# Log-sum-exp over heads: the range check as a chain of reduces, and a new split of the heads of a whole tile

## The chip, the cores and the metric

The kernel runs on one core of a Trainium2 chip. The engines are named TensorE (PE in the profile, with PEld for its weight loads), VectorE (DVE), ScalarE (ACT), GpSimd (POOL) and SyncE (SP, which here only starts transfers). The metric is the device time of one execution in microseconds. Three runs of the kernel before gave 335.59, 335.64 and 335.72 us, so the median is 335.64 us.

## The reference

```python
def reference(x, bias):                       # x (8, 2048, 2048) f32, bias (8, 256) f32
    B, S, D = x.shape
    H = bias.shape[0]
    Dh = D // H
    x_heads = x.reshape(B, S, H, Dh).transpose(0, 2, 1, 3)
    x_heads = x_heads + bias[None, :, None, :]
    x_tiled = np.repeat(x_heads, 2, axis=2)
    mx = x_tiled.max(axis=-1, keepdims=True)
    lse = mx.squeeze(-1) + np.log(np.exp(x_tiled - mx).sum(axis=-1))
    return lse.astype(np.float32)
```

For each of the 16384 rows and 8 heads, the 256 numbers of the head get the head's bias, and the logarithm of the sum of their exponentials is wanted; every result is written twice side by side. The input is 134.2 MB and the output 1.05 MB, so nearly all traffic is the load of `x`.

The kernel sums exp(x + bias) without taking the maximum away first. A range check makes that safe: it looks whether every sum lies within a factor of 2^60 of one, and whether no bias is larger than 20 in size. If the check fails, a slow second pass (`all_again`) computes everything with the maximum; on this input the pass is skipped.

## The kernel before

**Tiles and buffers.** The work is cut into 64 tiles, eight per batch. A tile is two rows on each of 128 partitions: 128 x 2 x 2048 numbers, 2.1 MB. Four buffers `xb` hold two tiles each. Tiles 2 to 41 are loaded two at a time (4.2 MB, line 171), the others one at a time or in pieces (line 183), all by SP's queue in the order of the tiles. A buffer is loaded again once the last instructions that use it (`last_uses`) are done, so a load eight tiles ahead waits for a tile to be finished.

**Stages.** `STAGES` says how the heads of a tile are shared out. Tiles 0 to 53 are whole tiles in the mode `BULK`; tiles 54 to 56 are `MIXED`; tiles 57 to 63 are worked on in half tiles and smaller pieces.

**A whole tile** (`BULK`: `pe=3, acc=1, g0=4`) goes three ways:
- Heads 0 to 2: TensorE writes the bias into PSUM (`put_bias`, line 297: a matmul of ones with three bf16 parts of the bias) and adds `x` to it with a matmul by the identity (`late_heads`, line 356). ScalarE takes the exp. For head 0 it also sums (line 367, `one_ps`); heads 1 and 2 are written back to SBUF (line 374, `pair`).
- Head 3: ScalarE takes the exp of the bare `x`, and VectorE multiplies by exp(bias), which lies in PSUM in `w_ps` (line 424, 2 x 256 numbers a partition).
- Heads 4 to 7: GpSimd adds the bias in SBUF (`g_add`, line 406, 2 x 1024 numbers), and ScalarE takes the exp.

One exp on ScalarE covers heads 3 to 7 (`exp_inplace`, line 412, 2560 numbers). At the end one `tensor_reduce` on VectorE sums heads 1 to 7 of both rows (line 431, 3584 numbers into 14 sums). The sums of a batch land in a tile `R` (128 partitions x 128 numbers).

**Weighing** (`weigh`, line 447) is another form: one fused VectorE instruction multiplies a head of one row by exp(bias) and sums it, and a second, short one reads the sum out of the accumulator. Before the change only the mixed and the last tiles use it. In the last tiles GpSimd multiplies and folds one or two heads (`fold`, lines 463 and 471), and TensorE runs spare matmuls (`keep_warm`, line 347).

**Order.** The order of the instructions on each engine is the order in which the program emits them (`manual_schedule`). The loop over tiles emits TensorE's and GpSimd's part of tile t, then the second half of tile t-1 (`later`: exp, multiply, reduce, reload), then ScalarE's exps of the heads of tile t that TensorE made (`pe_part`).

**End of a batch.** One iteration after the batch's last sums, `finish` transposes `R` on TensorE (line 491) and ScalarE takes the logarithm (line 501). `how_far` checks the sums on VectorE: a `tensor_scalar` takes the bits of the sums as integers less the bits of 1.0 (line 512), and a `tensor_reduce` finds the largest absolute value (line 519). After the last batch `judge` reduces the nine columns of `far`, turns the column into a row with TensorE and reduces it to one number, which all engines read to decide on the second pass.

Of the kernel before, what the change touches and what calls it, by code (L numbers as in the profile page):

```python
# [11 lines left out]
I32 = mybir.dt.int32  # L12
# [20 lines left out]

BULK = dict(pe=3, acc=1, g0=4, late=True, fold=0)
MIXED = dict(pe=1, acc=1, g0=4, late=False, fold=0)
# [9 lines left out]
SPAN_BITS = 60 << 23  # L45
TOO_FAR = float(1 << 30)

# [15 lines left out]
def kernel(  # L63
# [37 lines left out]

    far = sb.tile([P, B + 1], F32, name="far")
    dist = sb.tile([P, P], F32, name="dist")
    b_far = sb.tile([1, 1], F32, name="b_far")
    all_far = sb.tile([P, 1], F32, name="all_far")
    verdict = sb.tile([1, 1], I32, name="verdict")

    R = [sb.tile([P, KB, H, NB], F32, name=f"R{b}") for b in range(B - 1)]
    R_last = sb.tile([P, H, NBLK, K], F32, name="R_last")
    res = sb.tile([H * NB, B - 1, P, KB, 2], F32, name="res")  # L110
# [125 lines left out]
    for i, c in enumerate(range(G0, D, MM)):  # L236
        spread(ps[i], c, c + MM)
        nc.vector.tensor_copy(b_rep[:, c - G0 : c - G0 + MM], ps[i])
    w_late = w_ps[:, 0 : G0 - W0]
    spread(w_late, W0, G0)  # L240
    nc.scalar.activation(out=w_late, in_=w_late, func=ACT.Exp)

    nc.vector.memset(far, 0.0)
    nc.vector.tensor_reduce(
# [6 lines left out]
    nc.vector.tensor_scalar(  # L251
        out=far[0:1, B : B + 1],
        in0=b_far,
# [10 lines left out]
    def other_factors():  # L264
        nc.scalar.activation(
            out=w_ps[:, G0 - W0 :], in_=b_rep[:, 0 : W2 - G0], func=ACT.Exp
        )
        nc.scalar.activation(out=w_sb, in_=b_rep[:, W1 - G0 :], func=ACT.Exp)
# [81 lines left out]

    def late_heads(m, t, got, sums):

# [12 lines left out]
        def pe_part():  # L365
# [14 lines left out]
            )  # L380
            on_x(t, act, [mms[-1]])

# [30 lines left out]

    def later(m, t, k0, k1, sums, add):

        h0 = m["pe"] if m["late"] else m["g0"]
        v = xts[t % NBUF][:, k0:k1, h0 * Dh : D]
        done = exp_inplace(t, v, add)
        if m["late"]:
            n = (m["g0"] - h0) * Dh  # L420
            f = v[:, :, 0:n]
            h0 = m["acc"]
            v = xts[t % NBUF][:, k0:k1, h0 * Dh : D]
            mul = nc.vector.tensor_tensor(  # L424
                out=f,
                in0=f,
                in1=each_row(w_ps, m["pe"] * Dh - W0, n, k1 - k0),
                op=ALU.mult,
            )
            done = on_x(t, mul, [done])  # L430
        red = nc.vector.tensor_reduce(  # L431
            out=sums[:, k0:k1, h0:H],
            in_=v.rearrange("p k (h j) -> p k h j", j=Dh),
            op=ALU.add,
            axis=mybir.AxisListType.X,
        )
        last_uses[t].append(on_x(t, red, [done]))

# [20 lines left out]
    def fold(t, k, h0, h1, sums, after):  # L459
# [49 lines left out]

    def how_far(b, sums):  # L510

        nc.vector.tensor_scalar(  # L512
            out=dist,
            in0=sums.bitcast(I32),
            scalar1=float(ONE_BITS),
            scalar2=None,
            op0=ALU.subtract,
        )
        nc.vector.tensor_reduce(  # L519
            out=far[:, b : b + 1],  # L520
            in_=dist,
            op=ALU.max,
            axis=mybir.AxisListType.X,
            apply_absolute_value=True,
        )

    def judge():
        nc.vector.tensor_reduce(
            out=all_far, in_=far, op=ALU.max, axis=mybir.AxisListType.X
        )  # L530
        row = w_ps[0:1, 0:P]
# [96 lines left out]
    for t in range(T):  # L628
# [74 lines left out]
    finish_last()  # L703
    how_far(B - 1, R_last.rearrange("p h n k -> p (h n k)"))
    again = judge() > SPAN_BITS
# [34 lines left out]
```

## Time and profile before

| what | value |
| --- | --- |
| median of three runs | 335.64 us |
| the profiled execution's own time | 335.89 us |
| its span | 334.0 us |
| mean granted TensorE clock | 0.895 of full speed |
| loads of x (queue q1): share of 16 engines' span | 95.5% |
| line 431, reduce of 3584 numbers: count, mean | 54, 3888 ns |
| line 424, multiply of 512 numbers: count, mean | 54, 678 ns |
| line 512, tensor_scalar of the check: count, mean | 7, 2640 ns |
| line 519, reduce of the check: count, mean | 8, 286 ns |
| line 406, GpSimd's add of 2048 numbers: count, mean | 57, 4536 ns |
| line 412, exp of 2560 numbers: count, mean | 54, 2346 ns |

The profile is of one execution. A row of a group gives its line, engine and operation, the tile written and the tile read, shapes, count, total and mean busy time, and the idle time of the engine ahead of it with what ended it. A row of the windows gives a stretch of the span, then for each engine the busy time and the number of instructions, then the granted TensorE clock, the busy share of the 16 DMA engines and the rate of the transfers. In the slices each digit is a fortieth of the span in tenths of busy time. The busy times of two neighbouring instructions on VectorE or ScalarE may overlap a little, so the distance from one start to the next is the better price of an instruction in a row of them.

### The profile page before, as it was taken

What the parts mean: (1) busy time and instruction counts of PE and PEld (TensorE: products, weight loads), DVE (VectorE), ACT (ScalarE), POOL (GpSimd) and SP (SyncE); (2) the same over time, 40 slices, a digit from 0 to 9 for tenths busy, and PEclk for the clock granted to TensorE, in tenths of its full rate; (3) what the DMA queues carried; (4) which work ended last, traced back from release to release, by engine and by line L of the source; (5) the groups of instructions that cost most, each with busy time, mean ns of one, the idle gap of its engine ahead of it and who ended that gap; (6) DMA issues with size and microseconds to landing.
All of it is one profiled execution on the core that took longest, in us unless ns stands there. A gap on an engine that the chain in (4) does not pass through costs nothing.

```text
span 334.0 us, 2450 instructions
## 1 busy us (share of the span) xinstructions
PE 271.2 (81%) x692; PEld 103.6 (31%) x692; DVE 305.5 (91%) x327; ACT 263.6 (79%) x426; POOL 287.6 (86%) x120
## 2 busy tenths in 40 slices
PE   6999999888796996769846899869995986829991
PEld 2333333323232332223312333323331331314560
DVE  2256779999999999999999999999999999999996
ACT  1176499889876998689847999958995799949991
POOL 7939997999999999999999999999999999446881
PEclk9977799979977998999995999969999699567996
DMA  8999999999999999999999999999999999999920
GB/s 313 442 440 436 440 426 413 420 440 436 440 432 438 421 424 424 436 436 437 432 431 424 424 432 420 432 426 426 426 429 426 428 418 420 423 420 415 388 77 18
DMA packets 8832, 135.44 MB, mean 406 GB/s; under 512 B 1041, under 2 KB 1425, under 8 KB 2417
## 3 DMA queue, kind: packets, MB, share of 16 engines
q1 hardware_dynamic: 8720, 135.27, 95.5%
q8 instruction: 5, 0.08, 0.1%
q14 instruction: 9, 0.07, 0.1%
q10 hardware_dynamic: 98, 0.01, 0.0%
HBM read 134.23 MB, written 1.05 MB: 405 GB/s over the span
## 4 chain that ended last, share of the span: by engine, by line
DVE 85%; PE 12%; ACT 1%; issue 1%; DMA 0%; DVEq 0%
DVE R L431 60%; DVE xb L424 9%; DVE xb L447 9%; DVE dist L512 5%; PE pair L356 4%; PE one_ps L356 2%; PE pair L297 2%; PE one_ps L297 1%; PE pair L232 1%; DVE far L519 1%; ACT xb L412 1%; DVE R_last L431 1%; DMA brow<-in_bias_dram 0%; DVE R_last L477 0%; ACT xb L374 0%
## 5 line engine op out<-in xcount | busy, mean ns | idle before, releaser
L406 POOL TENSOR_TENSOR xb<-xb,b_rep 128x2048 f32<-128x2048 f32 x57 | 257.4, 4536 | 21.8 <-DMA xb<-in_x_dram 21.8
L431 DVE TENSOR_REDUCE R<-xb 128x14 f32<-128x3584 f32 (+1 forms) x56 | 214.5, 3830 | 1.9
L412 ACT ACTIVATE xb<-xb 128x2560 f32<-128x2560 f32 (+5 forms) x77 | 157.5, 2057 | 3.8 <-POOL xb L406 3.8
L356 PE MATMUL pair<-xb,ident 128*128 128x512 f32 x216 | 114.8, 658 | 0.0
L356 PE MATMUL one_ps<-xb,ident 128*128 128x512 f32 x108 | 67.9, 714 | 4.6 <-DMA xb<-in_x_dram 4.6
L374 ACT ACTIVATE xb<-pair 128x1024 f32<-128x1024 f32 x54 | 55.9, 1035 | 18.8 <-PE pair L356 18.7
L356 PEld LDWEIGHTS pair<-xb,ident 128*128 128x128 f32 x216 | 46.4, 215 | 62.0 <-issue 62.0
L424 DVE TENSOR_TENSOR xb<-xb,w_ps 128x512 f32<-128x512 f32 x54 | 36.6, 678 | 16.7 <-ACT xb L412 16.7
L367 ACT ACTIVATE xb<-one_ps 128x256 f32<-128x256 f32 x108 | 40.3, 387 | 6.9 <-PE one_ps L356 6.7
L297 PEld LDWEIGHTS <-ones 3*128 3x128 bf16 (+1 forms) x192 | 17.1, 94 | 80.0 <-issue 70.7
L297 PE MATMUL one_ps<-b,ones 3*128 3x512 bf16 x49 | 18.6, 380 | 24.8 <-ACT xb L367 24.8
L297 PE MATMUL pair<-b,ones 3*128 3x512 bf16 x98 | 29.3, 378 | 0.0
L356 PEld LDWEIGHTS one_ps<-xb,ident 128*128 128x128 f32 x108 | 17.6, 205 | 26.5 <-issue 18.2
L501 ACT ACTIVATE res<-tp 32x1024 f32<-32x1024 f32 x7 | 7.1, 1014 | 21.4 <-PE tp L491 21.4
L332 PE MATMUL pair<-xb,ident 128*128 128x512 f32 (+1 forms) x36 | 21.0, 670 | 2.9 <-DMA xb<-in_x_dram 2.9
L367 ACT ACTIVATION_READ_ACCUMULATOR xb<-one_ps 128x1 f32 x108 | 23.1, 214 | 0.0
L447 DVE CUSTOM_DVE_ANT_0 xb<-xb,w_ps 128x256 f32<-128x256 f32 x61 | 22.4, 418 | 0.0
L491 PE MATMUL tp<-ident,R 128*32 128x128 f32 x28 | 6.4, 324 | 18.8 <-DVE R L431 18.8
L463 POOL TENSOR_TENSOR xb<-xb,w_sb 128x256 f32<-128x256 f32 (+1 forms) x13 | 10.0, 772 | 12.2 <-ACT xb L412 11.6
L512 DVE TENSOR_SCALAR dist<-R 128x128 f32<-128x128 int32 x7 | 18.5, 2640 | 0.0
L471 POOL TENSOR_TENSOR xb<-xb 128x128 f32<-128x128 f32 (+3 forms) x39 | 13.9, 356 | 3.1
L347 PE MATMUL tp<-ident 128*128 128x128 f32 x84 | 14.4, 313 | 0.0
(52 smaller groups left out, 110.3 us busy)
## 6 DMA issues: line engine op xcount, KB each, us to landing
xb<-in_x_dram SPq DMA_DIRECT2D x20, 4096.0 KB, 17.2
xb<-in_x_dram SPq DMA_DIRECT2D x17, 2048.0 KB, 17.2
xb<-in_x_dram SPq DMA_DIRECT2D x12, 1024.0 KB, 15.2
xb<-in_x_dram SPq DMA_DIRECT2D x4, 256.0 KB, 13.3
out_dram<-res SPq DMA_DIRECT2D x1, 896.0 KB, 6.8
xb<-in_x_dram SPq DMA_DIRECT2D x2, 384.0 KB, 15.2
xb<-in_x_dram SPq DMA_DIRECT2D x2, 128.0 KB, 6.4
out_dram<-res_last SPq DMA_DIRECT2D x1, 128.0 KB, 1.7
```

The costliest lines, as they stand in the source:

```text
L297: nc.tensor.matmul(p, lhsT=lhsT, rhs=each_row(b, h * Dh, Dh, K), start=i == 0, stop=False,)
L332: mm = nc.tensor.matmul(p, lhsT=ident, rhs=xts[t % NBUF][:, ka:kb, c : c + w], start=False, stop=True,)
L347: nc.tensor.matmul(tp[:, 0], lhsT=ident, rhs=ident, start=True, stop=True)
L356: mm = nc.tensor.matmul(p, lhsT=ident, rhs=xts[t % NBUF][:, :, h * Dh : (h + 1) * Dh], start=False, stop=True,)
L367: act = nc.scalar.activation(out=xts[t % NBUF][:, k, 0:Dh], in_=got[0][:, k * Dh : (k + 1) * Dh], func=ACT.Exp, accum_out=sums[:, k, 0:1],)
L374: act = nc.scalar.activation(out=xts[t % NBUF][:, :, Dh : m["pe"] * Dh].rearrange("p k (h j) -> p h k j", j=Dh), in_=got[-1].rearrange("p ...
L406: add = nc.gpsimd.tensor_tensor(out=v, in0=v, in1=each_row(b_rep, c - G0, D - c, k1 - k0), op=ALU.add)
L412: return on_x(t, nc.scalar.activation(out=v, in_=v, func=ACT.Exp), [after])
L424: mul = nc.vector.tensor_tensor(out=f, in0=f, in1=each_row(w_ps, m["pe"] * Dh - W0, n, k1 - k0), op=ALU.mult,)
L431: red = nc.vector.tensor_reduce(out=sums[:, k0:k1, h0:H], in_=v.rearrange("p k (h j) -> p k h j", j=Dh), op=ALU.add, axis=mybir.AxisListTy ...
L447: ttr = nc.vector.tensor_tensor_reduce(out=v, in0=v, in1=w, scale=1.0, scalar=0.0, op0=ALU.mult, op1=ALU.add, accum_out=dst,)
L512: nc.vector.tensor_scalar(out=dist, in0=sums.bitcast(I32), scalar1=float(ONE_BITS), scalar2=None, op0=ALU.subtract,)
```

## The change

**The heads of a whole tile.** `BULK` gets `g0=5`. GpSimd adds the bias of three heads, 5 to 7 (2 x 768 numbers), and no longer four. Heads 3 and 4 are now exp of the bare `x`, and both are weighed: four `weigh` instructions a tile (two rows by two heads) and their accumulator reads, in place of the one multiply. The one reduce of heads 1 to 7 becomes two: heads 1 and 2 ahead of the weighings (1024 numbers, waiting for ScalarE's exp of `pair` only), and heads 5 to 7 after them (1536 numbers). At the start `w_ps` gets the factors of heads 3 and 4 (512 columns and not 256); in the middle `other_factors` makes the rest. The mixed tiles and the last tiles are not changed.

**The check.** Every `R` has one more column at each end. `ends_of` replaces `how_far`: one reduce takes the largest bits of a batch's sums together with the right-hand end column, one the smallest together with the left-hand one, and they write them into the end columns of the next batch's `R`. So the extremes are carried from batch to batch, and there is no subtraction for each batch. `judge` takes the bits of 1.0 away once, by a matmul that puts them into the row and a second one that adds the extremes.

```diff
--- before.py
+++ after.py
@@ -31,7 +31,7 @@

-BULK = dict(pe=3, acc=1, g0=4, late=True, fold=0)
+BULK = dict(pe=3, acc=1, g0=5, late=True, fold=0)
 MIXED = dict(pe=1, acc=1, g0=4, late=False, fold=0)
 PROMPT_F1 = dict(pe=2, acc=2, g0=8, late=False, fold=1)
 PROMPT_F2 = dict(pe=2, acc=2, g0=8, late=False, fold=2)
@@ -43,7 +43,7 @@
 BIAS_MAX = 20.0
 ONE_BITS = 127 << 23
 SPAN_BITS = 60 << 23
-TOO_FAR = float(1 << 30)
+TOO_FAR = 3.0e38

 STAGES = [
     (0, (BULK,)),
@@ -99,14 +99,17 @@
     bparts = sb.tile([1, 3, CPE], BF16, name="bparts")
     brest = sb.tile([1, 2, CPE], F32, name="brest")

-    far = sb.tile([P, B + 1], F32, name="far")
-    dist = sb.tile([P, P], F32, name="dist")
     b_far = sb.tile([1, 1], F32, name="b_far")
-    all_far = sb.tile([P, 1], F32, name="all_far")
+    one_bits = sb.tile([1, 1], F32, name="one_bits")
+    ends = sb.tile([P, 2], F32, name="ends")
+    far = sb.tile([P, 1], F32, name="far")
     verdict = sb.tile([1, 1], I32, name="verdict")

-    R = [sb.tile([P, KB, H, NB], F32, name=f"R{b}") for b in range(B - 1)]
-    R_last = sb.tile([P, H, NBLK, K], F32, name="R_last")
+    NR = KB * H * NB
+
+    Rx = [sb.tile([P, 1 + NR + 1], F32, name=f"R{b}") for b in range(B)]
+    R = [r[:, 1 : 1 + NR].rearrange("p (k h n) -> p k h n", k=KB, h=H) for r in Rx[:-1]]
+    R_last = Rx[-1][:, 1 : 1 + NR].rearrange("p (h n k) -> p h n k", h=H, n=NBLK)
     res = sb.tile([H * NB, B - 1, P, KB, 2], F32, name="res")
     res_last = sb.tile([P, P, 2], F32, name="res_last")
     xbs = [sb.tile([P, KB, D], F32, name=f"xb{i}") for i in range(NBUF // TB)]
@@ -236,11 +239,14 @@
     for i, c in enumerate(range(G0, D, MM)):
         spread(ps[i], c, c + MM)
         nc.vector.tensor_copy(b_rep[:, c - G0 : c - G0 + MM], ps[i])
-    w_late = w_ps[:, 0 : G0 - W0]
-    spread(w_late, W0, G0)
+    W_LATE = BULK["g0"] * Dh
+    w_late = w_ps[:, 0 : W_LATE - W0]
+    spread(w_late, W0, W_LATE)
     nc.scalar.activation(out=w_late, in_=w_late, func=ACT.Exp)

-    nc.vector.memset(far, 0.0)
+    nc.vector.memset(Rx[0][:, 0:1], 1.0)
+    nc.vector.memset(Rx[0][:, 1 + NR :], 1.0)
+    nc.vector.memset(one_bits, float(ONE_BITS))
     nc.vector.tensor_reduce(
         out=b_far,
         in_=brow,
@@ -249,7 +255,7 @@
         apply_absolute_value=True,
     )
     nc.vector.tensor_scalar(
-        out=far[0:1, B : B + 1],
+        out=Rx[0][0:1, 1 + NR :],
         in0=b_far,
         scalar1=BIAS_MAX,
         scalar2=TOO_FAR,
@@ -263,7 +269,7 @@

     def other_factors():
         nc.scalar.activation(
-            out=w_ps[:, G0 - W0 :], in_=b_rep[:, 0 : W2 - G0], func=ACT.Exp
+            out=w_ps[:, W_LATE - W0 :], in_=b_rep[:, W_LATE - G0 : W2 - G0], func=ACT.Exp
         )
         nc.scalar.activation(out=w_sb, in_=b_rep[:, W1 - G0 :], func=ACT.Exp)

@@ -348,7 +354,7 @@
                 tp[:, 0], lhsT=ident, rhs=ident, start=True, stop=True
             )

-    def late_heads(m, t, got, sums):
+    def late_heads(m, t, got, sums, pe_done):


         mms = []
@@ -378,7 +384,7 @@
                 in_=got[-1].rearrange("p (h k j) -> p h k j", k=K, j=Dh),
                 func=ACT.Exp,
             )
-            on_x(t, act, [mms[-1]])
+            pe_done.append(on_x(t, act, [mms[-1]]))

         return pe_part

@@ -411,30 +417,33 @@
     def exp_inplace(t, v, after):
         return on_x(t, nc.scalar.activation(out=v, in_=v, func=ACT.Exp), [after])

-    def later(m, t, k0, k1, sums, add):
-
-        h0 = m["pe"] if m["late"] else m["g0"]
-        v = xts[t % NBUF][:, k0:k1, h0 * Dh : D]
-        done = exp_inplace(t, v, add)
-        if m["late"]:
-            n = (m["g0"] - h0) * Dh
-            f = v[:, :, 0:n]
-            h0 = m["acc"]
-            v = xts[t % NBUF][:, k0:k1, h0 * Dh : D]
-            mul = nc.vector.tensor_tensor(
-                out=f,
-                in0=f,
-                in1=each_row(w_ps, m["pe"] * Dh - W0, n, k1 - k0),
-                op=ALU.mult,
-            )
-            done = on_x(t, mul, [done])
+    def add_up(t, k0, k1, h0, h1, sums, after):
         red = nc.vector.tensor_reduce(
-            out=sums[:, k0:k1, h0:H],
-            in_=v.rearrange("p k (h j) -> p k h j", j=Dh),
+            out=sums[:, k0:k1, h0:h1],
+            in_=xts[t % NBUF][:, k0:k1, h0 * Dh : h1 * Dh].rearrange(
+                "p k (h j) -> p k h j", j=Dh
+            ),
             op=ALU.add,
             axis=mybir.AxisListType.X,
         )
-        last_uses[t].append(on_x(t, red, [done]))
+        last_uses[t].append(on_x(t, red, [after]))
+
+    def later(m, t, k0, k1, sums, add, pe_done):
+        xt = xts[t % NBUF]
+        h0 = m["pe"] if m["late"] else m["g0"]
+        done = exp_inplace(t, xt[:, k0:k1, h0 * Dh : D], add)
+        if m["late"]:
+            add_up(t, k0, k1, m["acc"], m["pe"], sums, pe_done[0])
+            for k in range(k0, k1):
+                for h in range(h0, m["g0"]):
+                    weigh(
+                        t,
+                        xt[:, k, h * Dh : (h + 1) * Dh],
+                        h,
+                        sums[:, k, h : h + 1],
+                        done,
+                    )
+        add_up(t, k0, k1, m["g0"], H, sums, done)

     def weigh(t, v, h, dst, after):
         c = h * Dh
@@ -473,7 +482,7 @@
             )
             on_x(t, done, [])

-        def add_up():
+        def add_fold():
             red = nc.vector.tensor_reduce(
                 out=sums[:, k, h0:h1],
                 in_=v[:, :, 0:FOLD],
@@ -482,7 +491,7 @@
             )
             on_x(t, red, [done])

-        return add_up
+        return add_fold

     def finish(b):

@@ -507,29 +516,40 @@
             in_=res.rearrange("q b p k r -> q b (p k r)"),
         )

-    def how_far(b, sums):
-
-        nc.vector.tensor_scalar(
-            out=dist,
-            in0=sums.bitcast(I32),
-            scalar1=float(ONE_BITS),
-            scalar2=None,
-            op0=ALU.subtract,
-        )
+    def ends_of(b):
+
+
+        bits = Rx[b].bitcast(I32)
+        if b < B - 1:
+            low = Rx[b + 1][:, 0:1].bitcast(I32)
+            high = Rx[b + 1][:, 1 + NR :].bitcast(I32)
+        else:
+            low, high = ends[:, 0:1], ends[:, 1:2]
         nc.vector.tensor_reduce(
-            out=far[:, b : b + 1],
-            in_=dist,
-            op=ALU.max,
+            out=high, in_=bits[:, 1:], op=ALU.max, axis=mybir.AxisListType.X
+        )
+        nc.vector.tensor_reduce(
+            out=low,
+            in_=bits[:, 0 : 1 + NR],
+            op=ALU.min,
             axis=mybir.AxisListType.X,
-            apply_absolute_value=True,
+            negate=b == B - 1,
         )

     def judge():
-        nc.vector.tensor_reduce(
-            out=all_far, in_=far, op=ALU.max, axis=mybir.AxisListType.X
-        )
+
+
         row = w_ps[0:1, 0:P]
-        nc.tensor.transpose(out=row, in_=all_far, identity=ident)
+        nc.tensor.matmul(row, lhsT=one_bits, rhs=ones, start=True, stop=False)
+        nc.vector.scalar_tensor_tensor(
+            out=far,
+            in0=ends[:, 1:2],
+            scalar=-2.0 * ONE_BITS,
+            in1=ends[:, 0:1],
+            op0=ALU.add,
+            op1=ALU.max,
+        )
+        nc.tensor.matmul(row, lhsT=far, rhs=ident, start=False, stop=True)
         nc.vector.tensor_reduce(
             out=verdict, in_=row, op=ALU.max, axis=mybir.AxisListType.X
         )
@@ -634,10 +654,11 @@
             m = modes_of(t)[k0]
             add = None
             heads = []
+            pe_done = []
             if c0 == 0:
                 bias_here = bias_there
             if m["late"]:
-                pe_part = late_heads(m, t, bias_here, sums)
+                pe_part = late_heads(m, t, bias_here, sums, pe_done)
             else:
                 heads = add_x(m, t, k0, c0, c1, bias_here)

@@ -678,9 +699,11 @@
                             done,
                         )

-            def pool_part(t=t, m=m, k0=k0, k1=k1, sums=sums, add=add):
+            def pool_part(
+                t=t, m=m, k0=k0, k1=k1, sums=sums, add=add, pe_done=pe_done
+            ):
                 if add:
-                    later(m, t, k0, k1, sums, add)
+                    later(m, t, k0, k1, sums, add, pe_done)
                 if k1 == K:
                     reload(t)

@@ -695,13 +718,13 @@
         fb, at = divmod(t - 2, NBLK)
         if fb >= 0 and at == NBLK - 1:
             finish(fb)
-            how_far(fb, R[fb].rearrange("p k h n -> p (k h n)"))
+            ends_of(fb)
             if fb == B - 2:
                 store()
     flush(for_pe)
     flush(for_pool)
     finish_last()
-    how_far(B - 1, R_last.rearrange("p h n k -> p (h n k)"))
+    ends_of(B - 1)
     again = judge() > SPAN_BITS

     order.__exit__(None, None, None)
```

More of the change, by code (lines that the diff above doesn't have):

```diff
@@ L508, in store @@
         )
-    def how_far(b, sums):
-        nc.vector.tensor_scalar(
-            out=dist,
-            in0=sums.bitcast(I32),
-            scalar1=float(ONE_BITS),
-            scalar2=None,
-            op0=ALU.subtract,
+    def ends_of(b):
[7 more added lines that the diff above has]
+            out=high, in_=bits[:, 1:], op=ALU.max, axis=mybir.AxisListType.X
         )
         nc.vector.tensor_reduce(
-            out=far[:, b : b + 1],
-            in_=dist,
-            op=ALU.max,
+            out=low,
+            in_=bits[:, 0 : 1 + NR],
+            op=ALU.min,
             axis=mybir.AxisListType.X,
-            apply_absolute_value=True,
+            negate=b == B - 1,
         )
     def judge():
-        nc.vector.tensor_reduce(
-            out=all_far, in_=far, op=ALU.max, axis=mybir.AxisListType.X
-        )
-        row = w_ps[0:1, 0:P]
-        nc.tensor.transpose(out=row, in_=all_far, identity=ident)
+        row = w_ps[0:1, 0:P]
+        nc.tensor.matmul(row, lhsT=one_bits, rhs=ones, start=True, stop=False)
[6 more added lines that the diff above has]
+            op1=ALU.max,
+        )
+        nc.tensor.matmul(row, lhsT=far, rhs=ident, start=False, stop=True)
         nc.vector.tensor_reduce(
```

## The prediction

> **What bounds the kernel now.** I read the page first (busy shares, chain of work), then the groups with forms kept apart, VectorE's timeline around the changed instructions, the windows by stage, and the waits of the DMA queue.
>
> The page: its span, busy shares, slices and chain.
>
> ```profile
> span 334.0 us, 2450 instructions
> PE 271.2 (81%) x692; PEld 103.6 (31%) x692; DVE 305.5 (91%) x327; ACT 263.6 (79%) x426; POOL 287.6 (86%) x120
> DVE  2256779999999999999999999999999999999996
> DMA  8999999999999999999999999999999999999920
> DVE 85%; PE 12%; ACT 1%; issue 1%; DMA 0%; DVEq 0%
> L406 POOL TENSOR_TENSOR xb<-xb,b_rep 128x2048 f32<-128x2048 f32 x57 | 257.4, 4536 | 21.8 <-DMA xb<-in_x_dram 21.8
> ```
>
> VectorE is on 85% of the chain and full from slice 7 on, yet the DMA row is full as well: two resources run nearly level. The timeline (start, duration) prices VectorE's steps; the last line is GpSimd's.
>
> ```profile
> 163.78 0.68 DVE L424 TENSOR_TENSOR xb<-xb,w_ps 128x512 f32<-128x512 f32 x1
> 164.49 3.89 DVE L431 TENSOR_REDUCE R<-xb 128x14 f32<-128x3584 f32 x1
> 168.29 0.68 DVE L424 TENSOR_TENSOR xb<-xb,w_ps 128x512 f32<-128x512 f32 x1
> ...
> 263.37 4.57 DVE L512 TENSOR_SCALAR dist<-R 128x128 f32<-128x128 int32 x1
> ...
> 292.46 0.42 DVE L447 CUSTOM_DVE_ANT_0 xb<-xb,w_ps 128x256 f32<-128x256 f32 x1
> 292.80 0.08 DVE L447 DVE_READ_ACCUMULATOR2_ANT R<- 128x1 f32 x1
> 292.80 2.28 DVE L431 TENSOR_REDUCE R<-xb 128x8 f32<-128x2048 f32 x1
> 295.00 0.41 DVE L447 CUSTOM_DVE_ANT_0 xb<-xb,one_ps 128x256 f32<-128x256 f32 x1
> ...
> 263.32 4.54 POOL L406 TENSOR_TENSOR xb<-xb,b_rep 128x2048 f32<-128x2048 f32 x1 [0.36 <-DMA xb<-in_x_dram]
> ```
>
> A whole tile costs VectorE 168.29 - 163.78 = 4.51 us. L512 lasts 4.57 us here and ends (267.94) just after the GpSimd add beside it (267.86); with GpSimd idle the same form took 227 ns (the groups' row for R_last). So the check's tensor_scalar waits for GpSimd, 2.64 us in the mean of seven. A weighing (L447) starts 0.34 us before what follows, its accumulator read included.
>
> The windows by stage (busy by engine, granted clock, DMA share, GB/s) and the DMA queue's own waits:
>
> ```profile
> 6.00:42.00 36.00, 36.00 (x79) 12.88 (x77) 19.62 (x12) 17.46 (x29) 29.33 (x8) 0.81 1.02 438
> 42.00:200.00 158.00, 128.43 (x314) 47.05 (x313) 154.88 (x73) 134.10 (x203) 145.37 (x33) 0.93 1.00 431
> 205.00:290.00 85.00, 69.03 (x163) 25.58 (x163) 84.34 (x39) 72.81 (x111) 79.96 (x18) 0.89 1.00 424
> 305.00:319.00 14.00, 14.00 (x64) 7.41 (x63) 13.97 (x85) 14.00 (x33) 11.81 (x28) 1.00 1.01 385
> 319.00:334.00 15.00, 7.73 (x39) 4.50 (x38) 11.74 (x71) 8.32 (x26) 6.38 (x13) 0.83 0.05 17
> ...
> SPq L171 <- DVE R L431: 178.7, 17, 21.8
> ```
>
> While the queue is deep (6 to 42) the loads run at 438 GB/s; later, when each load waits for VectorE to free its buffer, at 431 and 424. The last bytes land near 319.3 (one-microsecond windows: 111 GB/s in 319:320, nothing after), and the span ends 14.7 us later: work queued behind VectorE. Loads set a floor 3 to 6 us below today's; the backlog holds the rest.
>
> **VectorE per whole tile.** Removed: 4.51 us. Added: a reduce of 1024 elements, four weighings, a reduce of 1536. The reduce rows (3888 ns for 3584, 2284 for 2048) give 1.044 ns an element, so 1.21 and 1.75 us; a reduce is followed 0.08 us before its end (292.80 to 295.00 is 2.20 for 2.28), so 1.13 + 1.67. Four weighings: 4 x 0.34 = 1.36. Sum 4.17 us. Upper bound, nothing overlapping: 4 x (0.418 + 0.084) + 2.96 = 4.97. I take 4.17: the mixed tiles run these very forms in a row, six weighings and a reduce in 295.00 - 290.76 = 4.24 us.
>
> [...]
>
> **The check, seven times on the way.** Removed: 2.64 + 0.29 us. Added: two reduces of 128 elements, like L519 at 286 ns: 0.57 us, or 0.41 overlapped. No such row is a tensor_scalar, and the reduces of 3584 run at 3.89 us beside GpSimd's adds all along, so I expect no hold; if there were one, it would cost at most today's 2.6.
>
> Sum for eight tiles: before 8 x 4.51 + 2.9 = 39.0 us, after 8 x 4.17 + 0.5 = 33.9. Eight tiles are 16.78 MB, 38.3 us at 438 GB/s. So VectorE falls from level with the loads to 12% below them, and the loads are late next.
>
> **GpSimd.** Rows of 2048 (4536 ns) and 512 elements (1279, line 463) give 3.45 us for 1536: 9.1 us per pair become 6.9, off the path, and the exp behind them starts sooner. Tiles 54 to 56 keep theirs.
>
> **ScalarE and TensorE** keep their work. In steady runs a tile costs ScalarE 3.84 us (timeline, 45.45 to 49.29) and TensorE as much at full clock, under the 4.8 us of a load. The start takes a 512-column spread and exp for 256: two passes of some 0.5 us more on TensorE, 0.2 on ScalarE. That delays the first tiles by up to 1.0 us, hidden by the eight loads issued ahead (to about 41 us); uncovered it would cost 1.0. At the middle the exp of the other factors shrinks by 256 columns (-0.2). The three memsets lie before VectorE's first wait of 9.1 us. Where each batch ends, ScalarE's Ln waits 21.4 us and TensorE's transposes 18.8 us over the seven for VectorE's sums (the waits); these shrink, off the path. The change adds one wait: the reduce of heads 1 and 2 comes first on VectorE and waits for their exp. ScalarE runs that ahead of the exp of heads 3 to 7, for which the weighings wait, so nothing behind it is held longer. On SP the loads keep their order; their wait is still for VectorE's last reduce.
>
> **The end of the program.** Last check: two reduces for 0.23 + 0.29, a scalar_tensor_tensor for the 162 ns reduce, one more one-row matmul issued ahead of the last wait. Sum within 0.1 us either way; I take nothing.
>
> **Sum.** Loads: 158 us at 438 for 431 saves 2.5; 85 us at 424 saves 0 (its load form may be slower) to 2.7, I take 1.4. So the last landing comes 3.9 earlier (2.5 to 5.2). After it, 14.7 us today. The floor is 4.1 (transpose of the last sums at 329.94 to the end) + exp 0.40 + weighing 0.43 = 5.0. Above that I put 1.1 for three accumulating exps flushed last (0.36 each) and 0.9 for a lag of half a tile: 7.0. ScalarE's half tile in the last stages takes 2.09 us (line 412 at 311.38 and 313.47), a load of it 2.5 to 2.7, so a lag shrinks; up to 10 us may remain, since GpSimd's last add (4.5) puts ScalarE behind at tile 56. Saved there: 7.7 (4.7 to 9.7). Total 11.6; against the profiled execution's 335.89 us (span 334.0 + 1.9 around it; 0.25 over the median of 335.64): **324.3 us**. Its own range: 321.0 (5.2 + 9.7) to 328.7 (2.5 + 4.7), or 320 if the loads reach the 440 of the best slices.
>
> **Rivals.**
> 1. The backlog at the end is ScalarE's and TensorE's own (both are busy 14.00 of 14.00 us from 305 to 319), and only the loads gain: 335.9 - 3.9 = 332.0. For it: those windows. Against: before 300 us ScalarE idles 4.4 us for a transpose that waits for VectorE's sums.
> 2. No change: loads are full already (share 1.00), and the lag stays: 335.6. Against: 438 is sustained for 36 us.
> 3. Slower: VectorE stays the bound because weighings don't overlap in whole tiles. It decides from 0.48 us a weighing, where eight tiles pass 38.3 us; with reduces unoverlapped too, 8 x 4.97 + 0.6 = 40.4, 1.4 us more per eight tiles, 6.75 times: 345.3. For it: no row has a weighing beside a long GpSimd add. Against: beside GpSimd's short ones (295.6 to 297.5) it keeps 0.34. [...]
> 4. TensorE, idler, is granted less clock: at 0.72 a tile took 6.5 us at the start (with six extra bias matmuls). At 5.1 us a tile instead of 4.87: 54 x 0.23 = 12 us, 348. Against: a slow stretch makes it busy, and its clock came back each time (0.93 in the mean).
>
> **Numbers.** Forecast 0.71, rivals 0.14, 0.05, 0.07, 0.03. Range 320.5 to 332: the forecast's own and the first rival. Within 0.2% is about what this measurement can tell from no change; faster 0.86 (the forecast, the first rival, a fifth of the second), same 0.04, slower 0.10.
>
> **What would show it.** Reduces near 1.2 and 1.75 us; weighings 0.34 apart beside adds of 3.4 us; no VectorE row over 0.3 us in the check; idle time of VectorE put down to ScalarE; loads at 436 or more from 42 to 200; the last landing at 314 to 317; the end 6 to 9 us behind it. Wrong if VectorE stays full to the end, if loads stay at 431, or if TensorE's clock falls under 0.8.

## The result and the profile after

The changed kernel takes 330.09 us (median), the kernel before 335.63 us in the same series. The ratio is 0.990, with a 95% interval from 0.985 to 0.995: faster, by about 1%. A second comparison gave 0.987 (0.981 to 0.994). Most executions of the changed kernel take 329.9 to 330.2 us and a few 333.8 to 334.1; most of the kernel before take 335.4 to 335.9 and a few 330.7 to 331.1, which is why the ratio stands nearer to one than the medians alone (0.983); no profile of the rarer kind exists for either kernel, so what sets them apart stays open. The forecast was 324.3 us.

The profiled execution takes 330.09 us with a span of 327.9 us, against 335.89 and 334.0. From the page of the changed kernel: span and busy shares, the slices of VectorE and of the transfers, the queues of instruction transfers (packets, MB, share), the shares of the chain.

```profile
span 327.9 us, 2891 instructions
PE 275.9 (84%) x695; PEld 104.0 (32%) x695; DVE 274.2 (84%) x761; ACT 264.6 (81%) x426; POOL 229.1 (70%) x120
DVE  1356779999899969688996998959899997989986
DMA  8999999999999999999999999999999999999984
q8 instruction: 5, 0.08, 0.1%
q14 instruction: 12, 0.10, 0.1%
DMA 43%; PE 21%; DVE 20%; ACT 13%; POOL 1%; issue 0%; SPq 0%; DVEq 0%
```

VectorE's share of the chain fell from 85% to 20%, and the loads have 43%: the bound has moved as forecast. VectorE now runs 761 instructions and no longer 327. The groups with forms kept apart, and VectorE's timeline in a whole tile:

```profile
L421 DVE TENSOR_REDUCE R<-xb 128x6 f32<-128x1536 f32 x54 | 94.5, 1750 | 0.0
L421 DVE TENSOR_REDUCE R<-xb 128x4 f32<-128x1024 f32 x54 | 65.5, 1213 | 22.6 <-ACT xb L380 22.6
L528 DVE TENSOR_REDUCE R<-R 128x1 int32<-128x129 int32 x7 | 1.9, 277 | 0.0
...
155.28 0.42 DVE L456 CUSTOM_DVE_ANT_0 xb<-xb,w_ps 128x256 f32<-128x256 f32 x1
155.62 0.08 DVE L456 DVE_READ_ACCUMULATOR2_ANT R<- 128x1 f32 x1
155.62 0.42 DVE L456 CUSTOM_DVE_ANT_0 xb<-xb,w_ps 128x256 f32<-128x256 f32 x1
...
156.30 2.88 DVE L421 TENSOR_REDUCE R<-xb 128x6 f32<-128x1536 f32 x2
159.43 0.42 DVE L456 CUSTOM_DVE_ANT_0 xb<-xb,w_ps 128x256 f32<-128x256 f32 x1
```

The weighings start 0.34 us apart; a tile costs 159.43 - 155.28 = 4.15 us. The windows by stage, with the columns as before:

```profile
6.00:42.00 36.00, 36.00 (x79) 12.62 (x78) 19.81 (x46) 17.62 (x29) 23.12 (x9) 0.86 1.02 437
42.00:200.00 158.00, 133.84 (x318) 48.35 (x316) 139.32 (x339) 135.24 (x206) 109.79 (x32) 0.91 1.00 431
205.00:290.00 85.00, 67.77 (x153) 23.74 (x151) 77.61 (x194) 72.82 (x111) 63.82 (x18) 0.86 1.00 423
305.00:319.00 14.00, 11.70 (x54) 6.55 (x53) 12.04 (x71) 13.34 (x33) 10.70 (x25) 1.00 0.90 345
319.00:334.00 15.00, 4.63 (x24) 2.43 (x23) 5.73 (x34) 5.06 (x17) 3.89 (x8) 0.93 0.26 62
```

VectorE, ScalarE and GpSimd all have idle time from 42 to 200, and the loads still run at 431 GB/s. From 305 to 319 they are slower than before (345 for 385), and bytes still move after 319. Most of those bytes are the store of the output, which shares the queue, so the windows alone do not give the end of the loads; the landing times further down do, and by them the loads end later than before, not earlier. Two steps of the chain and two rows of TensorE's timeline show where that is felt:

```profile
295.73 20.88 DMA xb<-in_x_dram
316.62 1.71 ACT xb L418
...
314.19 0.70 PE L338 MATMUL pair<-xb,ident 128*128 128x256 f32 x2 [1.31 <-DMA xb<-in_x_dram]
316.65 0.70 PE L338 MATMUL pair<-xb,ident 128*128 128x256 f32 x2 [0.68 <-DMA xb<-in_x_dram]
```

The load that lands at 316.62 is the last row of tile 62; 11.2 us of work follow it to the end of the span. I use the matmul on that row as the mark of the late loads from here on, and call it the mark.

The sum of it, from the landing times in the traces: the last load of x lands at 318.3 us before and at 322.0 us after (3.7 later); from there to the end it is 15.8 us before and 5.9 us after (9.8 less, from the unrounded times). 9.8 - 3.7 = 6.1 us, the difference of the spans.

### The profile page after: what moved, and what is told of

It is laid out like the page before. It is cut to its first block, busy times and chain, and to the rows that moved or that the text cites. A ratio compares the mean times of both kernels' runs of the same rounds, so it can differ in the third digit from the quotient of the medians.

```text
span 327.9 us, 2891 instructions
## 1 busy us (share of the span) xinstructions
PE 275.9 (84%) x695; PEld 104.0 (32%) x695; DVE 274.2 (84%) x761; ACT 264.6 (81%) x426; POOL 229.1 (70%) x120
## 4 chain that ended last, share of the span: by engine, by line
DMA 43%; PE 21%; DVE 20%; ACT 13%; POOL 1%; issue 0%; SPq 0%; DVEq 0%
DMA xb<-in_x_dram 43%; DVE R L421 11%; ACT xb L418 9%; PE pair L362 8%; DVE xb L456 8%; PE one_ps L362 5%; PE pair L303 3%; PE one_ps L303 2%; ACT xb L380 2%; POOL xb L412 1%; PE pair L235 1%; ACT res L510 1%; ACT xb L373 1%; PE tp L500 1%; DMA brow<-in_bias_dram 1%; PE w_ps L235 1%
## 5 line engine op out<-in xcount | busy, mean ns | idle before, releaser
L412 POOL TENSOR_TENSOR xb<-xb,b_rep 128x1536 f32<-128x1536 f32 (+1 forms) x57 | 199.0, 3507 | 82.6 <-DMA xb<-in_x_dram 82.6
L421 DVE TENSOR_REDUCE R<-xb 128x4 f32<-128x1024 f32 (+1 forms) x111 | 163.7, 1503 | 23.4 <-ACT xb L380 22.6
L362 PE MATMUL pair<-xb,ident 128*128 128x512 f32 x216 | 119.4, 682 | 0.0
L456 DVE CUSTOM_DVE_ANT_0 xb<-xb,w_ps 128x256 f32<-128x256 f32 x277 | 100.1, 416 | 17.8 <-ACT xb L418 17.7
L362 PEld LDWEIGHTS pair<-xb,ident 128*128 128x128 f32 x216 | 47.7, 221 | 64.3 <-issue 64.3
L362 PEld LDWEIGHTS one_ps<-xb,ident 128*128 128x128 f32 x108 | 17.2, 201 | 39.4 <-DMA xb<-in_x_dram 24.5
L456 DVE DVE_READ_ACCUMULATOR2_ANT R<- 128x1 f32 x305 | 25.2, 83 | 0.0
L353 PE MATMUL tp<-ident 128*128 128x128 f32 x84 | 13.7, 302 | 0.0
L353 PEld LDWEIGHTS tp<-ident 128*128 128x128 f32 x84 | 11.1, 200 | 3.5 <-issue 3.1
L393 ACT ACTIVATE xb<-pair 128x256 f32<-128x256 f32 x33 | 12.0, 370 | 0.0
L456 DVE CUSTOM_DVE_ANT_0 xb<-xb,one_ps 128x256 f32<-128x256 f32 x27 | 10.6, 414 | 1.0 <-ACT xb L418 1.0
```

The source lines that it names most:

```text
L353: nc.tensor.matmul(tp[:, 0], lhsT=ident, rhs=ident, start=True, stop=True)
L362: mm = nc.tensor.matmul(p, lhsT=ident, rhs=xts[t % NBUF][:, :, h * Dh : (h + 1) * Dh], start=False, stop=True,)
L393: act = nc.scalar.activation(out=xts[t % NBUF][:, k, h * Dh : (h + 1) * Dh], in_=p, func=ACT.Exp, accum_out=sums[:, k, h : h + 1],)
L412: add = nc.gpsimd.tensor_tensor(out=v, in0=v, in1=each_row(b_rep, c - G0, D - c, k1 - k0), op=ALU.add)
L421: red = nc.vector.tensor_reduce(out=sums[:, k0:k1, h0:h1], in_=xts[t % NBUF][:, k0:k1, h0 * Dh : h1 * Dh].rearrange("p k (h j) -> p k h j" ...
L456: ttr = nc.vector.tensor_tensor_reduce(out=v, in0=v, in1=w, scale=1.0, scalar=0.0, op0=ALU.mult, op1=ALU.add, accum_out=dst,)
```

## The experiments

The forecast had 3.9 us from faster loads, and the trace shows 3.7 us from later ones. My first theory was that the loads are full already, at 431 GB/s, and that the late rows come from the deep queue of loads, which lets the 16 DMA engines drift apart. Rivals: the loads are held by VectorE or by the buffers; the check or the split alone does it; the delay is chance. Only after the first four runs came the theory that the rest tests: one DMA engine is put behind by the transfers that fetch VectorE's longer program.

### One part alone

The chained check with the old split:

```diff
-BULK = dict(pe=3, acc=1, g0=5, late=True, fold=0)
+BULK = dict(pe=3, acc=1, g0=4, late=True, fold=0)
...
-            add_up(t, k0, k1, m["acc"], m["pe"], sums, pe_done[0])
-            for k in range(k0, k1):
-                for h in range(h0, m["g0"]):
-                    weigh(
...
+            n = (m["g0"] - h0) * Dh
+            f = xt[:, k0:k1, h0 * Dh : h0 * Dh + n]
+            mul = nc.vector.tensor_tensor(
...
+            add_up(t, k0, k1, m["acc"], H, sums, done)
```

> The chained check alone; the heads stay as before (GpSimd adds four heads, one multiply of 512 numbers and one reduce of 3584 on VectorE). My theory: the loads, at 431 GB/s from 42 us on in both kernels, are the bound as soon as VectorE needs less than their 38.9 us for eight tiles. Here VectorE needs 8 x 4.51 + 0.5 = 36.6 us, so nearly the whole gain should be here already: 329.5 to 331.5 us, VectorE's idle time in whole tiles put down to ScalarE or the loads, loads at 431 from 42 to 200 us. Rival, the parts add up (VectorE still sets the pace): the check is worth 16.5 of 26 us of VectorE's saved time, so about two thirds of the gain, 332 to 332.5 us. Rival, the check is off the path: 335.6.

Measured: 326.07 us (325.75 to 326.44), ratio 0.975 (0.969 to 0.982). That is 3.4 us below the expected range, and faster than the full change. From its page, its windows (42 to 200) and TensorE's timeline (the mark):

```profile
span 324.1 us, 2458 instructions
PE 269.8 (83%) x695; PEld 102.5 (32%) x695; DVE 290.0 (89%) x329; ACT 266.3 (82%) x426; POOL 287.3 (89%) x120
q14 instruction: 9, 0.07, 0.1%
...
42.00:200.00 158.00, 131.01 (x310) 47.66 (x310) 149.05 (x74) 135.28 (x205) 145.22 (x33) 0.91 1.00 431
...
312.84 0.70 PE L338 MATMUL pair<-xb,ident 128*128 128x256 f32 x2 [0.75 <-DMA xb<-in_x_dram]
```

The loads have the same rate, but the mark is 3.8 us earlier than in the full change (312.84 for 316.65), and so is the end (324.1 for 327.9). The last load of x lands at 318.1 us, as early as in the kernel before (318.3): the whole gain here is work that no longer stands behind it. VectorE is busier (290.0 for 274.2 us): its busy time is not what delays the loads.

The new split with the old check:

```diff
...
-    ends_of(fb)
+    how_far(fb, R[fb].rearrange("p k h n -> p (k h n)"))
...
```

> The new split of the heads alone, with the old check. VectorE needs 8 x 4.15 us plus the check, whose tensor_scalar should still wait for GpSimd's add (now 3.5 us long, so 1.5 to 2.6 us each): 35 to 36.1 us for eight tiles, under the 38.9 of the loads. My theory: nearly the whole gain here too, 329.5 to 331.5 us, though the waits at line 512 are still there. Rival, the parts add up: a third of the gain, 333.5 to 334 us.

Measured: 329.95 us, ratio 0.989 (0.982 to 0.997), as expected. The old `tensor_scalar` of the check still takes up to 2549 ns beside GpSimd's shorter adds (227 with GpSimd idle in the kernel before), and the mark is late again. The instructions of its line (least, median and largest duration in ns, first and last start) and TensorE's timeline:

```profile
L516 DVE TENSOR_SCALAR dist<-R x7: 217/1184/2549, 65.4 to 297.9; 128x128 f32<-128x128 int32 x7
...
316.60 0.70 PE L333 MATMUL pair<-xb,ident 128*128 128x256 f32 x2 [0.69 <-DMA xb<-in_x_dram]
```

So the lateness belongs to the split. Either part alone brings VectorE under the loads (busy for 149.1 and 145.8 of the 158 us from 42 to 200). The check alone gains 9.5 us, the split alone 5.6, both 5.5.

### The buffers, and the same kernel again

Three buffers of two tiles in place of four, with the reload of a tile moved later in the order:

```diff
-NBUF = 8
+NBUF = 6
...
-                    reload(t)
+                    for_load.append(lambda: reload(t))
```

> The changed kernel with three buffers of two tiles and not four (and the reload of a tile behind the exps of its half tiles, which only matters in the last tiles). In the changed kernel the loads are queued 24 us deep (median from issue to landing) and the last one or two of the 16 DMA engines end some 3.5 us after the others, which holds back the last row of tile 62 to 316.6 us. A third buffer less takes 9.7 us out of the queue. Theory that the spread of the engines comes from the deep queue: the rows of tile 62 land together by about 314 us and the time is 327 to 329.5 us. Rival, the spread has nothing to do with depth and the loads are still never short: 330.1 within 0.5. Rival, the queue runs dry: loads under 425 GB/s from 42 to 200 us and over 335 us.

Measured: 341.48 us, ratio 1.021 (1.014 to 1.028). The windows show a queue that ran dry, which is another effect from the start on:

```profile
6.00:42.00 36.00, 36.00 (x78) 12.98 (x79) 19.03 (x46) 17.78 (x29) 23.22 (x9) 0.87 0.99 421
42.00:200.00 158.00, 130.54 (x304) 47.28 (x303) 136.81 (x329) 130.97 (x198) 105.89 (x31) 0.90 0.98 414
```

This run doesn't serve its purpose: a loss of rate covers what was to be seen, so it says nothing on the theory of the deep queue. It does show that three buffers, with the reload placed so, are not enough.

> The changed kernel once more, on the chip of the three others. 14 of 18 runs took 329.9 to 330.2 us and four took 333.8 to 334.1; of the kernel before 15 took 335.4 to 335.9 and three 330.7 to 331.1. Theory: two ways of running that an execution falls into, not the chip; both should come up again in some runs. If they belong to the chip, all runs here are of one kind. In this profile I look at the spread of the last loads: a landing of the last row of tile 62 near 314 us should go with about 327 us, near 316.6 with 330, later with 334.

Measured, with no edit: 330.07 us (329.92 to 330.30), ratio 0.987 (0.981 to 0.994); the mark at 316.73, with a time near 330 as expected. The lateness is not chance. No time near 334 came up, so that part of the expectation was not tested.

### Instructions added alone, removed alone

To the chained check with the old split, eight memsets of one element in each whole tile on VectorE. The kernel leaves out the sum of head 7 there:

```diff
...
-            add_up(t, k0, k1, m["acc"], H, sums, done)
+            add_up(t, k0, k1, m["acc"], H - 1, sums, done)
+            for i in range(8):
+                nc.vector.memset(scratch[:, 8 * (t % 8) + i : 8 * (t % 8) + i + 1], 1.0)
...
```

> The chained check with the old split of the heads (326.1 us), and in each whole tile eight one-element memsets more on VectorE, some 430 instructions in all, about as many as the new split adds. Left out to make room: the sum of head 7 of whole tiles (the reduce has 3072 numbers, 0.53 us less; the cells keep 1.0). VectorE's time stays about 4.5 us a tile. Theory: the new split costs 4 us because VectorE's longer program has to be fetched, by transfers on one of the DMA engines that the loads keep full; that engine falls behind and the last loads wait for it. Then this kernel shows 3 or so more instruction transfers than check_only (9 there), a late last row of tile 62 (about 316.5 and not 313 us) and 329 to 331 us. Rival, the split costs 4 us through what its instructions do (weighings, GpSimd's shorter adds): 326.1 within 0.7.

Measured: 331.54 us (329.59 to 333.70), ratio 0.988 (0.980 to 0.997), 5.5 us more than without the memsets and 0.5 us above the expected range. The profile is of the longest execution. From its page and TensorE's timeline:

```profile
span 331.8 us, 2902 instructions
PE 278.3 (84%) x695; PEld 106.8 (32%) x695; DVE 270.6 (82%) x769; ACT 266.4 (80%) x426; POOL 287.5 (87%) x120
q14 instruction: 12, 0.10, 0.1%
...
316.65 1.22 PE L341 MATMUL pair<-xb,ident 128*128 128x256 f32 x2 [0.76 <-DMA xb<-in_x_dram]
```

VectorE is less busy than without them (270.6 for 290.0 us), runs 769 instructions like the full change, and the mark is at 316.65 like there. The matmul takes 1.22 us and not 0.70. The windows say why, first of this kernel and then of the full change:

```profile
316.00:319.00 3.00, 2.35 (x6) 1.27 (x7) 2.72 (x16) 2.89 (x10) 2.22 (x5) 0.53 0.59 169
319.00:322.00 3.00, 3.00 (x8) 1.23 (x8) 2.97 (x19) 1.79 (x4) 2.69 (x6) 0.50 0.94 208
```

```profile
316.00:319.00 3.00, 2.35 (x11) 1.36 (x11) 2.80 (x16) 2.97 (x10) 2.30 (x5) 1.00 0.60 171
319.00:322.00 3.00, 3.00 (x17) 1.89 (x17) 3.00 (x20) 3.00 (x9) 2.69 (x6) 1.00 0.94 208
```

The granted clock fell to 0.5 in this execution just as TensorE had waited for the late row, and the work behind it took 15.2 us and not 11.2. In the full change the same wait was followed by no fall, so the wait alone doesn't bring it; what does stays open.

From the full change, the four weighings and their four reads replaced by one multiply of 1024 numbers. The kernel leaves out the sums of heads 3 and 4 in whole tiles:

```diff
-            for k in range(k0, k1):
-                for h in range(h0, m["g0"]):
-                    weigh(
...
+            v = xt[:, k0:k1, h0 * Dh : m["g0"] * Dh]
+            w = each_row(w_ps, h0 * Dh - W0, (m["g0"] - h0) * Dh, k1 - k0)
+            mul = nc.vector.tensor_tensor(out=v, in0=v, in1=w, op=ALU.mult)
...
```

> The changed kernel (330.1 us) with three VectorE instructions a whole tile and not ten: one multiply of 1024 numbers (some 1.2 us) in place of four weighings and their four accumulator reads (1.36 us). Left out: the sums of heads 3 and 4 of whole tiles (the cells keep 1.0). GpSimd, ScalarE and TensorE do what they do in the changed kernel, and VectorE's time a tile stays within 0.2 us of it. Theory of the longer program: the instruction transfers fall back to about 9, the last row of tile 62 comes at about 313 us, 325.5 to 327 us. Rival, the rest of the split costs the 4 us: 330.1 within 0.5.

Measured: 326.94 us, ratio 0.977 (0.969 to 0.985), as expected. From its page and TensorE's timeline:

```profile
span 324.9 us, 2524 instructions
PE 270.6 (83%) x695; PEld 102.7 (32%) x695; DVE 263.3 (81%) x391; ACT 264.7 (81%) x426; POOL 229.0 (70%) x120
q14 instruction: 10, 0.08, 0.1%
...
313.67 0.70 PE L340 MATMUL pair<-xb,ident 128*128 128x256 f32 x2 [0.79 <-DMA xb<-in_x_dram]
```

So the number of instructions moves the mark in both directions. VectorE's busy time does not: 11 us less than in the full change go with an earlier mark here, 4 us less went with the same late one above.

### The loads without the work

In whole tiles only the loads stay, and one small VectorE reduce that frees the buffer:

```diff
...
+            if m["late"]:
+                red = nc.vector.tensor_reduce(
+                    out=sums[:, 0:K],
+                    in_=xt.rearrange("p k (h j) -> p k h j", j=Dh)[:, :, :, 0:8],
...
+                last_uses[t].append(on_x(t, red, [loads[t, 0, 0]]))
...
+                continue
...
```

> The changed kernel with nearly all work of the 54 whole tiles left out: TensorE, ScalarE and GpSimd do nothing there, and VectorE takes the largest of eight numbers a head, so a buffer is free at once. Theory: 431 GB/s from 42 to 200 us is the loads' own rate; here too 430 to 433 from 42 to 200 and 423 to 425 from 205 to 290. Rival, the rate of the first 36 us (438) can be held when buffers come free early, as my prediction took it: 436 or more, and the whole kernel 3 to 4 us shorter than the best of the others.

Measured: 325.77 us, in a single run. Its span and its windows by stage:

```profile
span 324.0 us, 989 instructions
6.00:42.00 36.00, 4.10 (x5) 1.01 (x5) 4.49 (x12) 0.58 (x1) 2.68 (x3) 1.00 1.02 437
42.00:200.00 158.00, 5.06 (x20) 2.17 (x20) 9.72 (x42) 5.15 (x7) 0.00 (x0) 1.00 1.00 431
205.00:290.00 85.00, 16.29 (x26) 4.99 (x26) 15.92 (x57) 14.62 (x22) 13.55 (x3) 1.00 1.00 424
```

With VectorE 6% busy the loads run at 437, then 431, then 424 GB/s, as in the full change within 1. These are the loads' own rates. The last load of x lands at 318.1 us, only 0.2 us earlier than in the kernel before (318.3), so there was next to nothing to gain from the loads. The kernel with the chained check alone ends at this floor (324.1 for 324.0 us).

### What one transfer of code costs

The records of the traces give each transfer's start, time and size, but neither its DMA engine nor the program that it belongs to. VectorE's code is taken to be the 8 KB transfers of the kind "instruction" whose number follows VectorE's instructions from run to run; in the changed kernel they take 0.325 to 0.333 us, the other 8 KB transfers of that kind 0.31 us, or 0.42 and more. The packets can be chained end to start: in the changed kernel, from 20 to 314 us, they make 16 chains, each taken for one DMA engine. There the transfers taken for VectorE's are:

```
start of transfer   its time   next packet (size, time)   usual time of that packet
 43.9 us            0.333 us   32 KB, 1.875 us            1.216 us
102.0               0.325      32 KB, 1.875               1.216
162.5               0.325      32 KB, 1.875               1.216
223.1               0.326      16 KB, 1.273               0.614
281.8               0.325       8 KB, 0.968               0.313
312.7               0.326       8 KB, 0.954               0.313
```

Each costs its chain about 0.33 + 0.66 = 0.98 us. The first four, whose chaining is plain, lie in one chain. The lateness adds up in the landings: each load of x steps its semaphore 16 times, and in the changed kernel the last step comes 0.39 us after the fifteenth for the load that lands at 160.5 us, 1.36 for the next one (behind the transfer at 162.5), 2.32 at 225.8 (behind the one at 223.1), 2.69 at 285.7 (behind the one at 281.8; 1.73 just ahead of it, as the fifteenth had come later too) and 3.62 for the marked row, which has fifteen steps by 312.98 and the last at 316.60. In the kernel before it is 0.23 us for that row. SyncE hands it on: in the full change it issues the last piece of x at 316.6 us, just as the marked row lands (316.60), and in the kernel before at 312.9, again as that row lands (312.91). Meanwhile the DMA engines are busy only for a share of 0.60 from 316 to 319 us (the window above). Two more kernels tested this in numbers: sixteen memsets a whole tile on VectorE in place of eight, and the kernel with one multiply with eight memsets a whole tile on GpSimd. For the first, some 1200 instructions were taken to make nine transfers ahead of the mark; seven more than the two of the chained check alone, at 0.97 us each, put it at 319.6 us, an estimate from the times above.

```diff
...
-            add_up(t, k0, k1, m["acc"], H - 1, sums, done)
-            for i in range(8):
+            add_up(t, k0, k1, m["acc"], H - 2, sums, done)
+            for i in range(16):
...
```

> The kernel with sixteen one-element memsets in each whole tile on VectorE (in place of eight; heads 6 and 7 are not summed in whole tiles, to pay for them). [...] So the matmul on that row starts at 319 to 320, the instruction queue shows 15 to 16 transfers, and the span is 330.5 to 331.5 (11.2 us behind the row), up to 335 if TensorE's clock falls there again. Rival, the lateness comes once, however many instructions there are (a step, or a state of the queue): row at 316 to 317, span 327.5 to 328.5.

```diff
...
         add_up(t, k0, k1, m["g0"], H, sums, done)
+        if m["late"]:
+            for i in range(8):
+                nc.gpsimd.memset(scratch[:, 8 * (t % 8) + i : 8 * (t % 8) + i + 1], 1.0)
```

> The kernel with one multiply in place of the weighings (heads 3 and 4 not summed in whole tiles; row of tile 62 at 313.67, 10 instruction transfers), and with eight one-element memsets in each whole tile on GpSimd, which does not set the end there. Theory: each engine's code comes through a DMA engine of its own, and the slowest of the 16 decides, so GpSimd's three or four further transfers (0.69 us each in the records so far) stay beside VectorE's three (0.97 each): 13 or 14 transfers, row at 313.5 to 314.3, span 324.8 to 325.6. Rival, the number of all transfers counts: row at 316 to 317, span 327 to 328.5. If GpSimd's code shares an engine with VectorE's, the row is at 315.8 to 316.5.

Measured, in a single run each: 332.96 us with sixteen memsets on VectorE, 327.07 us with eight on GpSimd. From the page and TensorE's timeline of the kernel with sixteen memsets on VectorE:

```profile
span 331.1 us, 3334 instructions
q14 instruction: 16, 0.13, 0.1%
...
319.83 0.70 PE L341 MATMUL pair<-xb,ident 128*128 128x256 f32 x2 [0.69 <-DMA xb<-in_x_dram]
```

From the page, the groups and TensorE's timeline of the kernel with eight memsets on GpSimd:

```profile
span 325.2 us, 2956 instructions
q14 instruction: 14, 0.11, 0.1%
L447 POOL MEMSET scratch<- 1x1 f32 x432 | 17.4, 89 | 0.0
...
313.95 0.70 PE L341 MATMUL pair<-xb,ident 128*128 128x256 f32 x2 [0.77 <-DMA xb<-in_x_dram]
```

Both marks and both spans fall where the theory had them, and each rival is out by 1.8 us or more. Ordered by VectorE's own transfers ahead of the mark:

| kernel | VectorE instructions | its transfers ahead of the mark | mark, us | span, us |
| --- | --- | --- | --- | --- |
| chained check alone | 329 | 2 | 312.84 | 324.1 |
| one multiply for the weighings | 391 | 3 | 313.67 | 324.9 |
| the same, 432 memsets on GpSimd | 391 | 3 | 313.95 | 325.2 |
| the change | 761 | 6 | 316.65 | 327.9 |
| eight memsets | 769 | 6 | 316.65 | 331.8 (clock 0.5) |
| sixteen memsets | 1201 | 9 | 319.83 | 331.1 |

From 2 to 9 transfers the mark moves 6.99 us, 1.0 us for each, and the end follows 11.2 to 11.3 us behind it wherever the clock held. Four more transfers with 432 instructions more on GpSimd hardly move it (0.3 us); on which engines they stand is not shown. Why the packet behind a transfer is lengthened by 0.66 us is open.

## Why the prediction was right and wrong

**VectorE's price: right.** Reduces of 1213 and 1750 ns (forecast 1.21 and 1.75), weighings 0.34 us apart, a tile 4.15 us (4.17), reduces of the check 277 ns. The third rival, weighings that don't overlap, falls: they start 0.34 us apart for 0.42 us of busy time. The larger number of instructions had another price: 432 more than with the chained check alone put the last rows 3.8 us back.

**The check: right.** No reduce was held: the seven pairs of reduces of 129 numbers on the way take at most 280 ns each. The `tensor_scalar` took from 217 to 2549 ns in the run with the split alone; why its time varies and a reduce's does not, no run shows.

**The end: right, a little too careful.** Forecast 14.7 us down to 7.0, a saving of 7.7. Measured by the landing times 15.8 down to 5.9, a saving of 9.8. The 14.7 counted from 319.3 us, where the last bytes move; those are the output's store, and the last load of x had landed at 318.3. The first rival, a backlog of ScalarE's and TensorE's own, falls, though its 332.0 us lie nearest to the time: ScalarE and TensorE have idle time from 305 to 319.

**The loads: wrong, and this is the step that failed.** "Loads: 158 us at 438 for 431 saves 2.5; 85 us at 424 saves 0 ... to 2.7, I take 1.4. So the last landing comes 3.9 earlier." The step took the rate of the first 36 us as one that the loads can hold, and put the fall to 431 down to waits for VectorE. The run with hardly any work shows the same 437, 431 and 424, and its last load of x lands only 0.2 us earlier than in the kernel before. The row behind the step, SyncE's waits for VectorE, did not mean that the loads ran short: after the change SyncE waits as long (173.0 us for 178.7), with the loads queued 24.0 us ahead for 17.2.

```profile
SPq L174 <- DVE R L421: 173.0, 17, 22.7
```

A warning was in the windows: a DMA share of 1.00 from 42 to 200 leaves no idle time in the DMA engines to fill. So the term is 0, the second rival's reason ("loads are full already") was right, and only its "the lag stays" was wrong.

**A term that was missing.** Beside the 0 comes a loss of 3.7 us that no step and no rival named: the transfers of VectorE's longer program. The rise from 2 to 10 VectorE instructions a tile was priced on VectorE alone, and not on the DMA engines, though loads filled these to 1.00. Forecast gain 3.9 + 7.7 = 11.6; measured -3.7 + 9.8 = 6.1; the miss of 5.5 us is 7.6 from the loads less 2.1 from the end. With the measured terms in place of both, the sum is 335.9 - 6.1 = 329.8. That the measured 330.09 us lies between 320.5 and 332 is luck: the forecast's own range ended at 328.7, and the rest was there for the first rival, whose reason was not the one found.

**TensorE's clock.** The fourth rival didn't decide: 0.901 in the mean for 0.895. But a short fall at the end cost 4 us in the run with eight memsets.

## What to carry to other kernels

Here the share of the DMA engines was 1.00 in the window and its rate was the loads' own; the better rate at the start was no reserve. The way to check that elsewhere is to take the work out and leave the loads. Where loads bound a kernel, count the instructions that a change adds on each engine: here some 125 on VectorE (872 more instructions in 7 more transfers) put the last rows back by 1.0 us, and the best version took the part of the change that adds next to none (329 instructions for 327), 326.07 us against 330.09. Read the end of the loads by the landing of the last one, not by the bytes of a window.

## What the runs showed of the hardware

- While the program runs, the profile shows transfers of the kind "instruction" among the loads: 12 of 8 KB and 5 of 16 KB in the full change. The 8 KB ones that are taken for VectorE's come six ahead of the mark with 761 VectorE instructions and nine with 1201, the first four of the full change in one chain; each cost that chain 0.33 us of its own and 0.66 us on the packet behind it. The five of 16 KB (1.02 to 1.09 us each in the full change, and some 0.5 us on the packet behind) come in every kernel that does the whole tiles, with 692 or 695 matmuls, and are taken for TensorE's; the kernel that leaves out the whole tiles' work has one, with 179, and its mark is hardly earlier (312.75 us for 312.84), so these don't add up as VectorE's do. Why is not shown; in the full change they lie in five different chains, but not beyond doubt.
- Loads of 32 KB packets run at 431 GB/s with all 16 engines full (1.216 us a packet), and only in the first 36 us at 437. What makes the start faster is open.
- In one execution of the kernel with eight memsets TensorE's granted clock was 1.00 from 313 to 316 us, 0.53 from 316 to 319 and 0.50 from 319 to 325, after a wait of 0.76 us for a late load, and the matmul on the marked row took 1.22 us for 0.70; in the full change the clock stayed at 1.00 after a wait of 0.68 us.
